# A decoder block in split fp32: another opening order, position rows as matmul rows, and other buffers for the compression's weights

## The chip, the cores and the metric

The kernel runs on one core of one Trainium2 chip. The metric is the device time of one execution in microseconds (us); where several executions were timed it is their median. The core has five engines that run side by side: PE (TensorE, matrix products), ACT (ScalarE), DVE (VectorE), POOL (GpSimd) and SP (SyncE), which here issues all the DMA transfers. A difference of about 0.5% is what repeated runs of this kernel can tell from none.

## What is computed

One layer of a decoder: 512 tokens of width 1024, batch 1. RMS norm, a token mixer, RMS norm and residual, then RMS norm, a SwiGLU channel mixer, RMS norm and residual. The mixer has two head groups that read one combined input projection: four heads of differential attention, and eight query heads (two key/value groups) of native sparse attention with a compressed, a selected and a window branch. Cut to what the change touches:

```python
h = rms_norm(x, attn_pre_norm[l])
proj = h @ w_in                      # dq, dk, dv, nq, kc, vc, ks, vs, kw, vw, gates
...
def compress_tokens(t, tok_idx, pos, w1, w2):
    blocks = t[:, :, tok_idx] + pos          # 31 blocks of 32 tokens, stride 16
    flat = blocks.reshape(..., 32 * 64)
    return silu(flat @ w1) @ w2
...
kc = compress_tokens(kc_tok, tok_idx, k_pos, k_w1, k_w2)
vc = compress_tokens(vc_tok, tok_idx, v_pos, v_w1, v_w2)
```

## The kernel before

**Numbers in two parts.** Most matrix products are done in fp32r on operands that are split in two: hi is the value rounded to fp32r, lo is the rest. A product is then three runs of matmuls: hi by hi, hi by lo, lo by hi. A weight tile is made in three steps: a DMA into a raw tile (`load_w`, L94), a copy on ACT to hi (`to_r`, L99 to L103, whi in the profile) and a subtraction on DVE to lo (`split_w`, L105 to L110, wlo). The raw, hi and lo tiles are 128 by 1024 and come from one shared pool with three buffers of each (`WB`).

**The planner.** The program states data flow; a planner orders the instructions of each engine at compile time by priority (mostly the order of the program text; attention heads are moved up by `HP` = 400) and by when it expects them to be ready, and gives out the buffers of each tag. Engines then run in that fixed order and wait on semaphores. So an edit can change the order of work that it does not mention.

**The opening (L164 to L254).** TensorE first does `WARM` = 12 matmuls on zeros, which no result uses. x comes transposed in eight pieces (`load_x`, L186 to L200): for each a DMA into xraw, an ACT copy scaled by the norm's gain to xh, a DVE operation that makes xl, an ACT square in place, and a DVE add into one of two running sums. Four "k" buffers hold the eight pieces. Among them the raw tiles of the first two weight tiles are loaded (`load_fm`, L202). Then come the constants (identities, masks, `sel`, L214 to L225), the rope tables, and the row scale: `ssum` sums the squares by matmuls, `rsqrt_mean` makes rstd, and `rb` spreads it over the rope tables (L231 to L243).

**The projections.** `fm_tile` (L257) splits a weight tile and does 24 matmuls of 512 columns: whi with the eight xh, whi with the eight xl, wlo with the eight xh. `rope_pair` (L268) does two such tiles and the rotation on DVE. `dv_half` (L327) makes half of the differential values, four tiles of 24 matmuls of 256 columns, evicted with rstd by ACT (L343) and DVE (L344); their PSUM tiles ("mm") have two buffers. `ORDER` (L46) lists the steps: the compressed pair C first, then v1, q0, q1, the value compression cv, n1, k0, the key compression ck, and so on, with the attention heads D0 to D3 and N0 to N7 among the later ones.

**The compression (`compress`, L375 to L458), run for values and keys.** The tokens come as cx, 128 rows (feature, and two neighbours) by 2 groups by 256. For each half of a block DVE adds the position values to 31 windows of 8 steps for each group (L398, 248 elements, reading every eighth element), ACT copies the sum to hi and DVE makes lo (L404 and L405). That gives 16 stationary operands of 124 columns: hi and lo, two groups, 31 blocks. The first weight matrix comes as four tiles through the shared pool (`load_w`, `split_w`), and 32 matmuls of 256 columns accumulate (L414). Two matmuls with `sel`, a stacked identity of 62 columns, add the hi rows to the lo rows and transpose (L420). SiLU and the second matrix follow.

**Attention.** Each softmax map takes its K operand from a "k" buffer (`load_k`, L305, two DMAs), and each head puts its transposed weights into a pair of "pt" tiles (`new_pt`, L504, two buffers of each).

Of the kernel before, what the change touches and what calls it, by code (L numbers as in the profile page):

```python
# [77 lines left out]
def hybrid_block_kernel(  # L78
# [26 lines left out]
    def split_w(raw, w=1024, lo_eng=None, hi_eng="a"):  # L105
        hi = wpool.tile([P, 1024], F32R, tag="hi", name="whi", bufs=WB[1])
        lo = wpool.tile([P, 1024], F32R, tag="lo", name="wlo", bufs=WB[2])
        to_r(hi_eng, hi[:, :w], raw[:, :w])
        (lo_eng or dve).tensor_tensor(lo[:, :w], raw[:, :w], f32(hi[:, :w]), OP.subtract)  # L109
# [28 lines left out]
    sel = T.tile([P, 2 * NCMP], F32, bufs=1, name="sel")  # L138
# [47 lines left out]
    def load_x(k):  # L186
        if k % 2 == 0:
            xraws[k // 2] = T.tile([P, 2, SEQ], F32R, tag="k", name="xraw", bufs=BUFS["k"])
        t = f32(xraws[k // 2][:, k % 2])
        nc.sync.dma_start(t, xT[:, k])  # L190
        h, l = sslot(f"xh{k}"), sslot(f"xl{k}")
        act.activation(h, t, AF.Copy, scale=gc[:, k:k + 1])
# [3 lines left out]
        act.activation(t, t, AF.Square)
        if sqs[k % 2] is None:
            sqs[k % 2] = t
        else:
            dve.tensor_tensor(sqs[k % 2], sqs[k % 2], t, OP.add)  # L200

    def load_fm(m):  # L202
        raws[m] = load_w(wf[m])

    first = 2 * FIRST_PAIR[ORDER.split()[0]]
    load_x(0)
    load_fm(first)
    for k in range(1, 4):
        load_x(k)
    load_fm(first + 1)  # L210
    for k in range(4, NK):
        load_x(k)
# [8 lines left out]
    dve.tensor_copy(sel, cst[:, 3 * P:3 * P + 2 * NCMP])  # L221
# [32 lines left out]
    dve.tensor_scalar_add(lam, lam, -LAM_INIT)  # L254


    def fm_tile(m, lo_eng=None):  # L257
        hi, lo = split_w(raws.pop(m), lo_eng=lo_eng, hi_eng="d" if m // 2 in HIF else "a")
        pt = ps("mm", f"fm{m}")
        seq = [(hi, xh), (hi, xl), (lo, xh)]  # L260
        n = 0
        for w, xx in seq:
            for k in range(NK):
                pe.matmul(pt, w[:, k * P:(k + 1) * P], xx[k], start=(n == 0), stop=(n == 3 * NK - 1))  # L264
# [110 lines left out]
    def compress(d, v, w1, w2, posd, w2cols):  # L375
# [14 lines left out]
        n2 = 2 * NCMP  # L390
        xs = []
        for half in range(2):
            st = tslot("cst", tag="c")
            stv = st[:, :8 * n2].rearrange("p (l g n) -> p l g n", l=8, g=GROUPS)
            for g in range(GROUPS):
                xg = xx[:, g * 256:(g + 1) * 256].rearrange("p (n l) -> p l n", l=8)
                xg = xg[:, :, half:half + NCMP]
                dve.tensor_tensor(stv[:, :, g], xg,  # L398
                                  pos[:, half * 8:half * 8 + 8].unsqueeze(2).to_broadcast([P, 8, NCMP]), OP.add)
            sv = st[:, :8 * n2].rearrange("p (l n) -> p l n", l=8)  # L400
            for q in range(2):
                hv = sslot("chl")[:, :8 * n2].rearrange("p (l s n) -> p l s n", l=4, s=2)
                sq = sv[:, 4 * q:4 * q + 4]
                act.activation(hv[:, :, 0], sq, AF.Copy)  # L404
                dve.tensor_tensor(hv[:, :, 1], sq, f32(hv[:, :, 0]), OP.subtract)  # L405
                xs.append(hv)
        for c in range(4):
            raw = load_w(w1[:, 4 * c:4 * c + 4].rearrange("(a d) l n -> d a (l n)", d=HALF))
            hi, lo = split_w(raw, hi_eng=hie("cv" if v else "ck"))
            for l in range(4):  # L410
                lh = 4 * c + l
                st = xs[lh // 4][:, lh % 4].rearrange("p s n -> p (s n)")
                for wi, w in enumerate((hi, lo)):
                    pe.matmul(hps[:2 * n2, :CMP_HIDDEN], st, w[:, l * 256:(l + 1) * 256],  # L414
                              start=(lh == 0 and wi == 0), stop=(lh == NLH - 1 and wi == 1))
        hs = tslot("chs", tag="c")
        act.activation(hs[:2 * n2, :CMP_HIDDEN], hps[:2 * n2, :CMP_HIDDEN], AF.Copy)
        pt = ps("tr", f"cht{v}")
        for j in range(2):
            pe.matmul(pt[:, j * 64:j * 64 + n2], hs[:2 * n2, j * P:(j + 1) * P], sel[:2 * n2], start=True, stop=True)  # L420
        ptv = pt[:, :P].rearrange("p (j n) -> p j n", j=2)[:, :, :n2]
        e = tslot("ce", tag="c")
        ev = e[:, :P].rearrange("p (j n) -> p j n", j=2)[:, :, :n2]
        act.activation(ev, ptv, AF.Exp, scale=-1.0)
        dve.tensor_scalar_add(ev, ev, 1.0)
        dve.reciprocal(ev, ev)
        if v == 0:
            hT = e[:, 256:256 + P].rearrange("p (j n) -> p j n", j=2)[:, :, :n2]
# [4 lines left out]
            pov = po[:, :n2].rearrange("p (g n) -> p g n", g=GROUPS)  # L433
            z = zero
            for t in (kch, kcl):
                act.activation(t[:, :, NCMP], z[:, :GROUPS], AF.Copy)
            act.activation(kch[:, :, :NCMP], pov, AF.Copy)
            dve.tensor_tensor(kcl[:, :, :NCMP], pov, f32(kch[:, :, :NCMP]), OP.subtract)
        else:
            hT = tslot("chT", tag="c")  # L440
            pool.memset(hT, 0.0)
            hv = hT.rearrange("p (j g r n) -> p j g r n", j=2, g=GROUPS, r=4)
            for j in range(2):
                for g in range(GROUPS):
                    src = (slice(None), j, slice(g * NCMP, (g + 1) * NCMP))
                    bc = [P, 4, NCMP]
                    dve.tensor_tensor(hv[:, j, g, :, :NCMP], ptv[src].unsqueeze(1).to_broadcast(bc),
                                      ev[src].unsqueeze(1).to_broadcast(bc), OP.mult)
# [536 lines left out]
```

## Time and profile before

| | us |
|---|---|
| runs shown: median of 3 (714.56, 717.43, 718.01) | 717.43 |
| profiled execution | 715.25 |
| its span, first to last instruction | 713.2 |
| PE busy | 683.7 |
| DVE busy | 488.3 |
| ACT busy | 295.9 |
| POOL busy | 63.1 |

The span is the part of the profiled execution between the first and the last instruction; 2.05 us of the time lie around it. Busy times are of one engine each and overlap. In the rows of the timeline the first number is the start in us, the second the time that the row covers; "xN" says that N instructions are merged; the brackets give the idle time of the engine ahead of it and what ended that. In the rows of the windows each engine has its busy time and its instructions (x), then come PEclk, the granted TensorE clock as a share of full speed, the share of DMA time used, and GB/s.

### The profile page before, as it was taken

To read this page: it belongs to the slowest core of one execution; us is meant where nothing else is said; L and a number is where in the kernel's file an instruction comes from. 1 tells how busy PE (TensorE), PEld (TensorE's weight loads), DVE (VectorE), ACT (ScalarE), POOL (GpSimd) and SP (SyncE) were. 2 spreads that over 40 slices of the span, in tenths; PEclk is the share of its full clock that TensorE was granted. 3 is DMA by queue.
4 is the path that set the end of the run, shared out by engine and by line. 5 is a ranking of instruction groups with operands and counts; after the bars stand their busy time and mean duration, and the time that the engine had idled before them with its cause. 6 is when DMAs were issued, how large, how long until landed. Compare 5 with 4: busy or idle time off the path is not lost.

```text
span 713.2 us, 9399 instructions
## 1 busy us (share of the span) xinstructions
PE 683.7 (96%) x3536; PEld 566.2 (79%) x3536; DVE 488.3 (68%) x803; ACT 295.9 (41%) x612; POOL 63.1 (9%) x74
## 2 busy tenths in 40 slices
PE   7999999999899998987899999999999999999995
PEld 4888878898788877866888888888888888888884
DVE  5777988876999995669586766867667672222227
ACT  7334444466689965435323233232232321121113
POOL 0000000111745434000000000000000000000000
PEclk8999999999999998999999999999999999999999
DMA  8347878551221300470022332223322222322303
GB/s 311 129 133 244 279 238 298 195 191 45 86 78 60 104 16 30 133 251 30 1 90 88 105 102 89 89 88 93 111 92 89 88 91 94 111 89 88 110 8 119
DMA packets 25980, 83.62 MB, mean 117 GB/s; under 512 B 3408, under 2 KB 4304, under 8 KB 25040
## 3 DMA queue, kind: packets, MB, share of 16 engines
q1 hardware_dynamic: 25936, 83.03, 35.0%
q8 instruction: 28, 0.46, 0.3%
q14 instruction: 16, 0.13, 0.1%
HBM read 73.06 MB, written 9.96 MB: 116 GB/s over the span
## 4 chain that ended last, share of the span: by engine, by line
PE 81%; DVE 12%; ACT 4%; issue 2%; DMA 1%; SPq 0%; DVEq 0%; ACTq 0%
PE gu L835 35%; PE acc L874 15%; PE fm L264 11%; PE tr L489 2%; PE mixp L664 2%; DVE nm L477 2%; PE dv L338 2%; PE vg L360 2%; PE avn L617 2%; PE sc L473 2%; PE sc L474 1%; PE mix L676 1%; PE av L540 1%; DVE p L533 1%; DVE ptl L494 1%
## 5 line engine op out<-in xcount | busy, mean ns | idle before, releaser
L109 DVE TENSOR_TENSOR wlo<-wraw,whi 128x1024 fp32r<-128x1024 f32 (+2 forms) x96 | 116.4, 1214 | 144.8 <-ACT whi L101 95.5
L101 ACT ACTIVATE whi<-wraw 128x1024 fp32r<-128x1024 f32 (+2 forms) x96 | 100.8, 1052 | 215.3 <-PE gu L835 92.0
L835 PE MATMUL gu<-hth,whi 128*128 128x512 f32 (+1 forms) x352 | 86.6, 388 | 0.0
L835 PE MATMUL gu<-htl,whi 128*128 128x512 f32 (+1 forms) x352 | 86.2, 385 | 0.0
L835 PE MATMUL gu<-hth,wlo 128*128 128x512 f32 (+1 forms) x352 | 85.6, 385 | 0.0
L835 PEld LDWEIGHTS gu<-hth,whi 128*128 128x128 f32 x352 | 65.0, 192 | 14.8 <-ACT hth L807 0.3
L835 PEld LDWEIGHTS gu<-htl,whi 128*128 128x128 f32 x352 | 64.3, 188 | 14.7
L835 PEld LDWEIGHTS gu<-hth,wlo 128*128 128x128 f32 x352 | 64.1, 188 | 14.7
L841 DVE RECIPROCAL silu<-silu 128x512 f32<-128x512 f32 (+1 forms) x24 | 74.0, 3085 | 0.7
L498 POOL TENSOR_TENSOR p<-p,l 128x384 f32<-128x384 f32 (+3 forms) x60 | 50.1, 862 | 145.0 <-DVE l L528 88.5
L874 PE MATMUL acc<-whi,ffl 128*128 128x512 f32 x144 | 56.0, 389 | 0.0
L874 PE MATMUL acc<-wlo,ffh 128*128 128x512 f32 x144 | 56.0, 389 | 0.0
L874 PE MATMUL acc<-whi,ffh 128*128 128x512 f32 x144 | 55.9, 389 | 0.0
L479 ACT ACTIVATE p<-sc,nm 128x128 f32<-128x128 f32 (+1 forms) x96 | 50.0, 528 | 10.2 <-DVE nm L477 9.8
L477 DVE TENSOR_REDUCE nm<-sc 128x1 f32<-128x128 f32 (+1 forms) x96 | 42.5, 482 | 11.0 <-PE sc L475 7.8
L264 PE MATMUL fm<-xh,whi 128*128 128x512 f32 x128 | 35.9, 419 | 4.8 <-ACT whi L101 2.9
L493 ACT ACTIVATE pth<-tr 128x384 fp32r<-128x384 f32 (+1 forms) x60 | 31.5, 526 | 17.4 <-PE tr L489 17.2
L473 PE MATMUL sc<-kst,qst 128*128 128x128 f32 (+2 forms) x96 | 35.6, 372 | 1.5 <-DVE pc L574 1.2
L494 DVE TENSOR_TENSOR ptl<-tr,pth 128x384 fp32r<-128x384 f32 (+1 forms) x60 | 34.8, 592 | 3.0 <-ACT pth L493 2.7
L489 PE MATMUL tr<-ident,p 128*128 128x128 f32 x200 | 33.6, 280 | 1.3 <-ACT pct L591 0.7
L264 PEld LDWEIGHTS fm<-xh,whi 128*128 128x128 f32 x128 | 24.9, 199 | 12.3 <-ACT whi L101 5.5
L264 PE MATMUL fm<-xl,whi 128*128 128x512 f32 x128 | 32.6, 391 | 0.0
(219 smaller groups left out, 1186.9 us busy)
## 6 DMA issues: line engine op xcount, KB each, us to landing
wraw<-in_wg SPq DMA_DIRECT2D x22, 512.0 KB, 3.3
wraw<-in_wu SPq DMA_DIRECT2D x22, 512.0 KB, 3.3
wraw<-in_wd SPq DMA_DIRECT2D x22, 512.0 KB, 3.3
wraw<-in_wf SPq DMA_DIRECT2D x16, 512.0 KB, 4.9
qk<-rope SPq DMA_DIRECT2D x7, 1024.0 KB, 5.9
kst<-qk SPq DMA_DIRECT2D x24, 256.0 KB, 4.4
qst<-qk SPq DMA_DIRECT2D x16, 256.0 KB, 2.7
wraw<-in_wo SPq DMA_DIRECT2D x8, 512.0 KB, 4.0
```

Source lines behind the costliest of these rows:

```text
L101: act.activation(dst, src, AF.Copy)
L109: (lo_eng or dve).tensor_tensor(lo[:, :w], raw[:, :w], f32(hi[:, :w]), OP.subtract)
L264: pe.matmul(pt, w[:, k * P:(k + 1) * P], xx[k], start=(n == 0), stop=(n == 3 * NK - 1))
L473: pe.matmul(sv, lhs, kk[:, 0, :w], start=True, stop=False)
L477: dve.tensor_reduce(nm, sv, AX.X, OP.max, negate=True)
L479: act.activation(pt, sv, AF.Exp, bias=nm, accum_out=l[:, i:i + 1])
L489: pe.transpose(tr[:, n * P:(n + 1) * P], pts[i][:, j * P:(j + 1) * P], ident)
L494: dve.tensor_tensor(ptl[:, sl], trv, f32(pth[:, sl]), OP.subtract)
L498: pool.tensor_tensor(p, p, l.to_broadcast(list(p.shape)), OP.mult)
L835: pe.matmul(pt, w_col(ww, k), hx[:, k, s0:s1], start=(n == 0), stop=(n == 3 * NK - 1))
L841: dve.reciprocal(sl, sl)
L874: pe.matmul(acc[i][c], a[f][:, i * P:(i + 1) * P], w[wi][:, c * SEQ:(c + 1) * SEQ], start=(first and n == 0), stop=(last and n == 2))
```

## The change

Three parts.

**The opening.** `load_x` now only loads, makes xh and, after pieces 1 to 3, issues three more matmuls of xh by itself into the warm tile, which no result uses. xl moves to `low_x`, the squares and their sums to a loop of their own, both behind all eight `load_x`. `load_fm` can split a tile when it is loaded, and `rope_pair` and the first two tiles do so. `WARM` goes from 12 to 20. `fm_tile` does whi with xh, wlo with xh, then whi with xl.

**Position rows.** The stationary operand has 128 columns: hi and lo, two groups, 31 blocks and one spare, in which the position values stand. The windows are no longer added to the position values: ACT copies them to hi and DVE makes lo (496 elements each), and the same is done for the position values (16 elements). `sel` now adds the position rows (31 and 95) to every block: it is built from the identity in three DVE operations.

**Weight tiles.** The operands of the compression lie in tiles of the tag "k" (in place of a "c" tile and four "s" tiles), its raw weight tiles too, and hi and lo are a "pt" pair from `new_pt`.

```diff
-WARM = 12
+WARM = 20
+WARMX = 3
...
-        h, l = sslot(f"xh{k}"), sslot(f"xl{k}")
+        h = sslot(f"xh{k}")
         act.activation(h, t, AF.Copy, scale=gc[:, k:k + 1])
-        dve.scalar_tensor_tensor(l, t, gc[:, k:k + 1], f32(h), OP.mult, OP.subtract)
         xh.append(h)
+        if 0 < k < 4:
+            for _ in range(WARMX):
+                pe.matmul(warm_ps, h[:, :P], h, start=True, stop=True)
+
+    def low_x(k):
+        t = f32(xraws[k // 2][:, k % 2])
+        l = sslot(f"xl{k}")
+        dve.scalar_tensor_tensor(l, t, gc[:, k:k + 1], f32(xh[k]), OP.mult, OP.subtract)
         xl.append(l)
+
+    def load_fm(m, split=False):
+        raws[m] = load_w(wf[m])
+        if split:
+            raws[m] = split_w(raws[m])
+
+    first = 2 * FIRST_PAIR[ORDER.split()[0]]
+    load_x(0)
+    load_fm(first, True)
+    for k in range(1, 4):
+        load_x(k)
+    load_fm(first + 1, True)
+    for k in range(4, NK):
+        load_x(k)
+    for k in range(NK):
+        low_x(k)
+    for k in range(NK):
+        t = f32(xraws[k // 2][:, k % 2])
         act.activation(t, t, AF.Square)
-        if sqs[k % 2] is None:
-            sqs[k % 2] = t
+        if k < 2:
+            sqs[k] = t
         else:
             dve.tensor_tensor(sqs[k % 2], sqs[k % 2], t, OP.add)
...
-    dve.tensor_copy(sel, cst[:, 3 * P:3 * P + 2 * NCMP])
+    n2 = GROUPS * NPAD
+    dve.tensor_tensor(sel, ident[:, :n2], ident[:, n2:], OP.add)
+    for r in (NCMP, n2 + NCMP):
+        dve.tensor_tensor(sel, sel, ident[:, r:r + 1].to_broadcast([P, n2]), OP.add)
...
-    def fm_tile(m, lo_eng=None):
-        hi, lo = split_w(raws.pop(m), lo_eng=lo_eng, hi_eng="d" if m // 2 in HIF else "a")
+    def fm_tile(m):
+        hi, lo = raws.pop(m)
         pt = ps("mm", f"fm{m}")
-        seq = [(hi, xh), (hi, xl), (lo, xh)]
+        seq = [(hi, xh), (lo, xh), (hi, xl)]
...
             if m not in raws:
-                load_fm(m)
+                load_fm(m, True)
...
-            st = tslot("cst", tag="c")
-            stv = st[:, :8 * n2].rearrange("p (l g n) -> p l g n", l=8, g=GROUPS)
-            for g in range(GROUPS):
-                xg = xx[:, g * 256:(g + 1) * 256].rearrange("p (n l) -> p l n", l=8)
-                xg = xg[:, :, half:half + NCMP]
-                dve.tensor_tensor(stv[:, :, g], xg,
-                                  pos[:, half * 8:half * 8 + 8].unsqueeze(2).to_broadcast([P, 8, NCMP]), OP.add)
-            sv = st[:, :8 * n2].rearrange("p (l n) -> p l n", l=8)
-            for q in range(2):
-                hv = sslot("chl")[:, :8 * n2].rearrange("p (l s n) -> p l s n", l=4, s=2)
-                sq = sv[:, 4 * q:4 * q + 4]
-                act.activation(hv[:, :, 0], sq, AF.Copy)
-                dve.tensor_tensor(hv[:, :, 1], sq, f32(hv[:, :, 0]), OP.subtract)
-                xs.append(hv)
+            st = T.tile([P, 2, SEQ], F32R, tag="k", name="cst", bufs=BUFS["k"])
+            st = st.rearrange("p q (l s g n) -> p (q l) s g n", s=2, g=GROUPS, n=NPAD)
+            xg = xx.rearrange("p (g n l) -> p l g n", g=GROUPS, l=8)[:, :, :, half:half + NCMP]
+            pg = pos[:, half * 8:half * 8 + 8].unsqueeze(2).to_broadcast([P, 8, GROUPS])
+            for dst, src in (((slice(0, NCMP)), xg), (NCMP, pg)):
+                act.activation(st[:, :, 0, :, dst], src, AF.Copy)
+                dve.tensor_tensor(st[:, :, 1, :, dst], src, f32(st[:, :, 0, :, dst]), OP.subtract)
+            xs.append(st)
         for c in range(4):
-            raw = load_w(w1[:, 4 * c:4 * c + 4].rearrange("(a d) l n -> d a (l n)", d=HALF))
-            hi, lo = split_w(raw, hi_eng=hie("cv" if v else "ck"))
+            raw = f32(T.tile([P, 2, SEQ], F32R, tag="k", name="w1", bufs=BUFS["k"])).rearrange("p a b -> p (a b)")
+            nc.sync.dma_start(raw, w1[:, 4 * c:4 * c + 4].rearrange("(a d) l n -> d a (l n)", d=HALF))
+            hi, lo = (t.rearrange("p a b -> p (a b)")[:, :1024] for t in new_pt())
+            to_r("a", hi, raw)
+            dve.tensor_tensor(lo, raw, f32(hi), OP.subtract)
...
-                    pe.matmul(hps[:2 * n2, :CMP_HIDDEN], st, w[:, l * 256:(l + 1) * 256],
+                    pe.matmul(hps[:, :CMP_HIDDEN], st, w[:, l * 256:(l + 1) * 256],
```

The remaining lines of the diff carry the width of 64 columns (two groups of 32) in place of 62 through the rest of `compress`.

More of the change, by code (lines that the diff above doesn't have):

```diff
@@ L137, in hybrid_block_kernel @@
     cmask_b = T.tile([P, NT * NPAD], BF16, bufs=1, name="cmask_b")
-    sel = T.tile([P, 2 * NCMP], F32, bufs=1, name="sel")
+    sel = T.tile([P, 2 * NPAD], F32, bufs=1, name="sel")
     valid = T.tile([P, 1], F32, bufs=1, name="valid")
@@ L190, in load_x @@
         nc.sync.dma_start(t, xT[:, k])
-        h, l = sslot(f"xh{k}"), sslot(f"xl{k}")
+        h = sslot(f"xh{k}")
         act.activation(h, t, AF.Copy, scale=gc[:, k:k + 1])
-        dve.scalar_tensor_tensor(l, t, gc[:, k:k + 1], f32(h), OP.mult, OP.subtract)
         xh.append(h)
-        xl.append(l)
+        if 0 < k < 4:
[5 more added lines that the diff above has]
+        dve.scalar_tensor_tensor(l, t, gc[:, k:k + 1], f32(xh[k]), OP.mult, OP.subtract)
+        xl.append(l)
+    def load_fm(m, split=False):
[14 more added lines that the diff above has]
+        t = f32(xraws[k // 2][:, k % 2])
         act.activation(t, t, AF.Square)
-        if sqs[k % 2] is None:
-            sqs[k % 2] = t
+        if k < 2:
+            sqs[k] = t
         else:
             dve.tensor_tensor(sqs[k % 2], sqs[k % 2], t, OP.add)
[L202 to L212, printed above, removed]
     cst = tslot("cst", tag="o")
@@ L389, in compress @@
         hps = ps(CMPT, f"cmp{v}")
-        n2 = 2 * NCMP
+        n2 = GROUPS * NPAD
         xs = []
         for half in range(2):
-            st = tslot("cst", tag="c")
-            stv = st[:, :8 * n2].rearrange("p (l g n) -> p l g n", l=8, g=GROUPS)
-            for g in range(GROUPS):
-                xg = xx[:, g * 256:(g + 1) * 256].rearrange("p (n l) -> p l n", l=8)
-                xg = xg[:, :, half:half + NCMP]
-                dve.tensor_tensor(stv[:, :, g], xg,
-                                  pos[:, half * 8:half * 8 + 8].unsqueeze(2).to_broadcast([P, 8, NCMP]), OP.add)
-            sv = st[:, :8 * n2].rearrange("p (l n) -> p l n", l=8)
-            for q in range(2):
-                hv = sslot("chl")[:, :8 * n2].rearrange("p (l s n) -> p l s n", l=4, s=2)
-                sq = sv[:, 4 * q:4 * q + 4]
-                act.activation(hv[:, :, 0], sq, AF.Copy)
-                dve.tensor_tensor(hv[:, :, 1], sq, f32(hv[:, :, 0]), OP.subtract)
-                xs.append(hv)
@@ L410, in compress @@
             for l in range(4):
                 lh = 4 * c + l
-                st = xs[lh // 4][:, lh % 4].rearrange("p s n -> p (s n)")
+                st = xs[lh // 8][:, lh % 8].rearrange("p s g n -> p (s g n)")
                 for wi, w in enumerate((hi, lo)):
-                    pe.matmul(hps[:2 * n2, :CMP_HIDDEN], st, w[:, l * 256:(l + 1) * 256],
+                    pe.matmul(hps[:, :CMP_HIDDEN], st, w[:, l * 256:(l + 1) * 256],
                               start=(lh == 0 and wi == 0), stop=(lh == NLH - 1 and wi == 1))
@@ L416, in compress @@
         hs = tslot("chs", tag="c")
-        act.activation(hs[:2 * n2, :CMP_HIDDEN], hps[:2 * n2, :CMP_HIDDEN], AF.Copy)
+        act.activation(hs[:, :CMP_HIDDEN], hps[:, :CMP_HIDDEN], AF.Copy)
         pt = ps("tr", f"cht{v}")
         for j in range(2):
-            pe.matmul(pt[:, j * 64:j * 64 + n2], hs[:2 * n2, j * P:(j + 1) * P], sel[:2 * n2], start=True, stop=True)
-        ptv = pt[:, :P].rearrange("p (j n) -> p j n", j=2)[:, :, :n2]
+            pe.matmul(pt[:, j * 64:j * 64 + n2], hs[:, j * P:(j + 1) * P], sel, start=True, stop=True)
@@ L422, in compress @@
+        ptv = pt[:, :P].rearrange("p (j n) -> p j n", j=2)
         e = tslot("ce", tag="c")
-        ev = e[:, :P].rearrange("p (j n) -> p j n", j=2)[:, :, :n2]
+        ev = e[:, :P].rearrange("p (j n) -> p j n", j=2)
         act.activation(ev, ptv, AF.Exp, scale=-1.0)
@@ L427, in compress @@
         if v == 0:
-            hT = e[:, 256:256 + P].rearrange("p (j n) -> p j n", j=2)[:, :, :n2]
+            hT = e[:, 256:256 + P].rearrange("p (j n) -> p j n", j=2)
             dve.tensor_tensor(hT, ptv, ev, OP.mult)
@@ L432, in compress @@
                 pe.matmul(po[:, :n2], w2t[:, j], hT[:, j], start=(j == 0), stop=(j == 1))
-            pov = po[:, :n2].rearrange("p (g n) -> p g n", g=GROUPS)
+            pov = po[:, :n2].rearrange("p (g n) -> p g n", g=GROUPS)[:, :, :NCMP]
             z = zero
@@ L444, in compress @@
                 for g in range(GROUPS):
-                    src = (slice(None), j, slice(g * NCMP, (g + 1) * NCMP))
+                    src = (slice(None), j, slice(g * NPAD, g * NPAD + NCMP))
                     bc = [P, 4, NCMP]
```

## The prediction

> **What bounds the kernel now.** I read the page's busy shares first, to see which engine is the bound, and then a table of stages (windows), to see where that engine stands idle or slow.
>
> ```profile
> span 713.2 us, 9399 instructions
> PE 683.7 (96%) x3536; PEld 566.2 (79%) x3536; DVE 488.3 (68%) x803; ACT 295.9 (41%) x612; POOL 63.1 (9%) x74
> core 0: us, PE busy (x) PEld busy (x) DVE busy (x) ACT busy (x) POOL busy (x), PEclk, DMA share, GB/s
> 0.00:7.65 7.65, 4.18 (x13) 1.43 (x13) 1.12 (x6) 3.42 (x6) 0.20 (x4) 0.99 0.69 201
> 7.65:15.49 7.84, 6.71 (x14) 3.94 (x15) 7.22 (x13) 7.84 (x14) 0.00 (x0) 0.57 1.05 397
> 15.49:23.50 8.01, 8.01 (x37) 6.67 (x37) 7.18 (x16) 5.37 (x8) 0.00 (x0) 1.00 0.74 265
> 23.50:38.35 14.85, 14.14 (x119) 13.94 (x120) 11.04 (x23) 3.74 (x9) 0.00 (x0) 1.00 0.24 72
> 38.35:110.00 71.65, 69.75 (x348) 58.77 (x347) 58.85 (x89) 31.20 (x47) 0.52 (x1) 1.00 0.71 235
> 110.00:180.00 70.00, 69.78 (x477) 61.55 (x475) 54.44 (x119) 37.73 (x108) 9.38 (x12) 1.00 0.50 174
> 180.00:260.00 80.00, 75.87 (x519) 61.34 (x519) 75.35 (x188) 65.07 (x196) 41.60 (x46) 0.98 0.24 77
> 260.00:350.00 90.00, 79.64 (x443) 67.91 (x442) 67.30 (x146) 43.43 (x103) 11.43 (x12) 0.94 0.26 88
> ```
>
> TensorE is busy 683.7 of 713.2 us, and no other engine above 488.3. So an edit is worth the TensorE idle or slow time that it removes, 29.5 us at most. The table says where that lies: before 7.65; in the opening, where ACT is busy all 7.84 us, DVE 7.22 and the granted clock is only 0.57; 0.71 us in 23.5 to 38.35; 1.9 us in 38.35 to 110. From 110 to 180 there is 0.2 us. The 14.5 us between 180 and 350 are in code that the diff leaves alone.
>
> **The opening.** Rows of the timeline, by time (start, us, engine, line, operation), then of the matmuls' line L264 and of the tile xraw (min/median/max ns, first and last start). Here x arrives in eight pieces, and the first two weight tiles (fm_a, fm_b: 48 matmuls) are multiplied with it.
>
> ```profile
> 1.22 4.18 PE L174 MATMUL warm<-warm 128*128 128x512 bf16 x12 [1.22 <-DVE zero L225]
> 7.65 0.79 PE L264 MATMUL fm<-xh,whi 128*128 128x512 f32 x1 [2.25 <-ACT whi L101]
> 8.02 1.93 ACT L192 ACTIVATE xh<-xraw,gc 128x512 fp32r<-128x512 f32 x3
> 10.38 1.04 ACT L101 ACTIVATE whi<-wraw 128x1024 fp32r<-128x1024 f32 x1
> 14.73 0.71 ACT L192 ACTIVATE xh<-xraw,gc 128x512 fp32r<-128x512 f32 x1
> 21.50 1.99 PE L264 MATMUL fm<-xh,wlo 128*128 128x512 f32 x8
> L264 PE MATMUL fm<-xh,whi x16: 389/628/793, 7.6 to 17.0; 128*128 128x512 f32 x16
> L264 PE MATMUL fm<-xl,whi x16: 389/389/389, 15.8 to 21.3; 128*128 128x512 f32 x16
> L264 PE MATMUL fm<-xh,wlo x16: 389/389/398, 19.5 to 23.1; 128*128 128x512 f32 x16
> L190 SPq DMA_DIRECT2D xraw<-in_xT x8: 328/432/738, 1.2 to 6.5; - x8
> DMA to landing us min/median/max: 3.5/5.8/6.3
> L196 ACT ACTIVATE xraw<-xraw x8: 613/614/633, 7.5 to 18.0; 128x512 f32<-128x512 f32 x8
> ```
>
> The last piece of x lands by 6.5 + 6.3 = 12.8 us, but ACT makes its xh only at 14.73 to 15.44: ACT spent five squares of 0.61 us ahead of it. From 15.8 on TensorE runs the 16 with xl, the 16 with wlo and, at 17.0, the last of the 16 of whi with xh: 33 of the 48, back to back until 23.49, 0.232 us each.
>
> The change puts the squares behind all of xh. ACT then needs after xh3 (third of the row at 8.02, now free to end near 9.6) one whi, 1.04, and four xh at some 0.62: 3.5 us. The second whi is begun at 10.38 today, so its data is there by then: started between 9.6 and 10.38, the four end between 13.1 and 13.9. The landing bound is 12.8 + 0.71 = 13.5, which I take: **13.5**. So xh is complete 1.9 us sooner, and the new order (whi with xh, wlo with xh, whi with xl) leaves more that needs no xl.
>
> How much is done by 13.5? TensorE has 5.85 us from 7.65, or 25 slots of 0.232. Nine go to the new warm matmuls (three after each of x1 to x3); some two are lost before xh1. That leaves 15, as many as before did by 15.8. The remaining 33 take 7.7 us again and end at 21.2 instead of 23.49: **-2.3 us**. Bounds: strictly in program order, only 8 of fm_a are done at 13.7 and 40 remain, 23.0 (-0.5); packed without a gap, 48 + 9 slots from 7.65 end at 20.9 (-2.6).
>
> This count needs TensorE at full clock from 7.65. The granted clock by windows:
>
> ```profile
> 4.12:7.53 3.41, 1.28 (x6) 0.39 (x4) 0.75 (x1) 1.71 (x3) 0.00 (x0) 1.00 0.95 339
> 7.53:10.95 3.42, 2.81 (x4) 1.14 (x4) 3.21 (x4) 3.42 (x7) 0.00 (x0) 0.50 1.04 407
> 10.95:14.36 3.41, 2.88 (x7) 2.31 (x8) 2.90 (x4) 3.41 (x7) 0.00 (x0) 0.50 1.06 398
> 307.91:311.32 3.41, 2.04 (x11) 1.66 (x10) 1.26 (x3) 1.18 (x4) 0.00 (x0) 1.00 0.94 292
> ```
>
> The clock is full from 4.12 to 7.53, in which TensorE is busy only 1.28 us, and halved for the next 6.8 us. A later window with 2.04 us busy (307.91) is in the full clock, and no drop follows it. The twelve warm matmuls end at 5.40: that fits seven at a cold 0.43 until 4.2 and five at some 0.22. With 20 of them thirteen follow the seven and end near 7.0: 2.8 us busy in that window, above the 2.04 that held. I take the clock as kept. [...]
>
> [...]
>
> **What the squares leave late.** The row scale rstd needs the sums of squares, and DVE is the tight engine:
>
> ```profile
> 19.03 1.89 DVE L200 TENSOR_TENSOR xraw<-xraw 128x512 f32<-128x512 f32 x3
> 23.32 0.84 PE L234 MATMUL ssum<-ones,xraw 128*128 128x1 f32 x7
> 34.95 0.48 DVE L344 SCALAR_TENSOR_TENSOR dv<-dv,rstd,dv 128x256 fp32r<-128x256 f32 x1
> 35.49 0.74 PE L338 MATMUL dv<-whi,xh 128*128 128x256 f32 x4 [0.71 <-DVE dv L344]
> L221 DVE COPY sel<-cst 128x62 f32<-128x62 f32 x1 | 0.2, 191 | 0.0
> ```
>
> Up to 20.9 DVE has the same xl, wlo, constants and adds in both kernels, plus two small operations for sel (about 0.4 us by the 191 ns row), and it is 91% busy (7.22 + 7.18 of 15.85). So the adds still end at 20.9 to 21.3. Before, the ssum matmuls waited for TensorE until 23.3. Now TensorE is ready at 21.2, when the adds are: the chain to rstd, rb and the eviction of dv moves with it, and the stall of 0.71 at 35.49 stays (bounds: gone, or grown by the whole 2.3). I take 0. ACT's eight squares, 4.9 us, lie behind xh from 13.5 beside two whi of wdv and end near 20.5, ahead of the last add.
>
> On SP the DMAs of x, weights and constants keep their order, and none gets a new wait. The new order within fm_tile holds whi for eight matmuls longer (1.9 us); its buffer is one of three, next needed two tiles (11 us) on: 0.
>
> **The compression.** It runs twice, once near 44 to 68 us and once near 85 to 98.
>
> ```profile
> L414 PE MATMUL cmp<-wlo,chl x32: 276/279/380, 60.4 to 96.9; 128*124 128x256 f32 x32
> 62.93 0.38 PE L414 MATMUL cmp<-wlo,chl 128*124 128x256 f32 x1 [0.53 <-DVE wlo L109]
> 91.39 0.73 PE L264 MATMUL fm<-xh,whi 128*128 128x512 f32 x2 [1.37 <-DVE chl L405]
> L398 DVE TENSOR_TENSOR cst<-cx,pos x8: 612/629/637, 44.3 to 88.1; 128x248 f32<-128x248 f32 x8
> L404 ACT ACTIVATE chl<-cst x8: 395/405/416, 45.5 to 89.0; 128x248 fp32r<-128x248 f32 x8
> L405 DVE TENSOR_TENSOR chl<-cst,chl x8: 404/410/418, 47.7 to 91.9; 128x248 fp32r<-128x248 f32 x8
> 103.48 4.96 SPq L310 DMA_DIRECT2D kst<-qk  x8
> 110.12 0.22 PE L473 MATMUL sc<-kst,qst 128*128 128x128 f32 x1
> ```
>
> Its matmuls keep their number and columns (124 stationary columns become 128), so their time. TensorE stood 0.53 us for a wlo and 1.37 us for a chl, both made by DVE. Per compression DVE did 4 x 0.63 + 4 x 0.41 = 4.2 us. Now it does two subtractions of 496 elements and two of 16. By sel's row (L221) 62 elements take 0.19, by L405 248 read in order take 0.41: 1.2 ns each above 0.12. By L398 248 read 8 apart take 0.63, 2.05 ns each. So 496 elements cost 0.7 or, read 8 apart as they are, 1.1 us, and 16 cost 0.15. Sum 2 x 1.1 + 2 x 0.15 = 2.5: some 1.6 us less on DVE. ACT did 4 x 0.405 = 1.6 and now does four copies, 1.6 to 2.6; it is 31.2 of 71.65 us busy, so that hides (without that cover, 1.0 us per compression).
>
> [...]
>
> The weight tiles move from the shared three-deep buffers to the four "k" and two pairs of "pt", idle until the first attention head's loads at 103.48. So they can be loaded and split early, and no projection tile waits behind them. I take 1.4 of the 1.9 us: **-1.4** (bounds 0 and -1.9; three quarters, since the larger stall is the one whose DVE work shrinks most).
>
> Sum: -2.3 - 1.4 + 0 = **-3.7 us**. The profiled execution took 715.25 (span 713.2 and 2.05 around it), so the sum by it is 711.5. It lies 2.2 below the median of 717.43 of the runs shown; I place the forecast from the middle of the two, 716.3: 716.3 - 3.7 = **712.6**.
>
> **The rivals.** *DVE keeps the opening.* If the planner lets the wlo of the next tiles ahead of the adds, rstd and rb come no earlier than before, DVE evicts dv at 34.95 as now, and the matmul at 35.49 starts at 35.49: 2.3 are given back as a longer stall. For it: DVE at 91%. Against: the ssum matmuls had 2.1 us to spare. Time 716.3 - 1.4 = 714.9.
>
> [...]
>
> *Slower: attention's K tiles come late.* They share the "k" buffers with the compression's two operand tiles and four weight tiles. Today all eight loads go out from 103.48, after the compression's last matmul at 96.9, and the scores begin at 110.12. The slack is 6.5 us: from the point where the planner ends the second compression later than 103.5, each us holds up the heads, whose DVE work is 75.35 of 80 us busy from 180 to 260 and cannot catch up. Put off behind one projection pair (48 x 0.232 = 11 us) it costs 11 - 6.5 = 4.5, about the gains; behind two, 22 - 6.5 = 15.5, and 716.3 - 3.7 + 15.5 = 728. The latter is this rival. Against: its tiles are ready earlier than before.
>
> *A new order downstream.* The planner orders all engines anew, and 14.5 us of idle between 180 and 350 can move. If a third goes: 707.8.
>
> **How the numbers follow.** Forecast 0.52, DVE 0.20, clock 0.08, late K 0.07, new order 0.13. The forecast's own range is 710.1 (715.25 - 2.6 - 1.9 - 0.7) to 715.8 (716.3 - 0.5). New order reaches below it, DVE with an unlucky start above it: all but 2 in 10 lies in 707 to 717.5. A measurement of this kernel tells about 0.5% from no change, here 3.6 us, so faster means below 713.8: four fifths of the forecast (0.41), the new order (0.13), half of clock (0.04) and a tenth of DVE (0.02) make 0.60. Slower, above 721, is late K: 0.07. The rest is 0.33.
>
> **What would show it.** xh complete near 13.5 and the last fm_b matmul near 21.2 (opening; 23 refutes it); granted clock 1.0 from 4 to 24; dv's last tile starting near 33.2 rather than 35.49 (DVE rival: 35.5); no idle above 0.5 us at the compression's matmuls; DVE's strided subtraction near 1.1 us; scores starting by 107 (late K: after 112). It would be wrong if TensorE idles more between 180 and 350 than the 14.5 us of now.

## The result, and the profile after

The changed kernel is slower: 725.75 us (median of 4 runs, 724.17 to 727.08) against 717.27 (4 runs), a ratio of 1.0124 with a 95% interval of 1.0095 to 1.0152. The forecast was 712.6 with a range of 707 to 717.5. The profiled execution took 724.17.

The page of the changed kernel, its span and busy shares:

```profile
span 722.2 us, 9431 instructions
PE 690.2 (96%) x3553; PEld 569.4 (79%) x3553; DVE 490.4 (68%) x797; ACT 299.9 (42%) x612; POOL 62.3 (9%) x74
```

Its windows, with the columns of the prediction's table (us, busy time of PE, PEld, DVE, ACT, POOL with instructions, granted clock, DMA share, GB/s; PEld is TensorE's loading of its stationary operands):

```profile
7.65:15.49 7.84, 7.73 (x34) 5.70 (x33) 5.44 (x7) 7.45 (x13) 0.00 (x0) 1.00 1.05 396
15.49:23.50 8.01, 7.78 (x40) 6.38 (x39) 8.01 (x22) 5.72 (x11) 0.00 (x0) 1.00 0.79 275
23.50:38.35 14.85, 14.85 (x120) 14.49 (x119) 12.62 (x28) 5.40 (x10) 0.00 (x0) 1.00 0.24 72
38.35:110.00 71.65, 69.09 (x338) 56.87 (x337) 54.98 (x78) 31.23 (x44) 0.53 (x1) 1.00 0.75 251
180.00:260.00 80.00, 72.22 (x477) 59.09 (x475) 67.72 (x171) 59.79 (x175) 33.64 (x38) 0.94 0.21 64
260.00:350.00 90.00, 82.05 (x450) 67.44 (x448) 71.00 (x151) 48.05 (x119) 15.84 (x16) 0.94 0.28 100
```

The opening does what it was meant to: the clock is full where it was 0.57, and the stall in 23.5 to 38.35 is gone. From 180 to 260 TensorE issues 477 matmuls where it issued 519. That is where the time went, and no line of the diff is there. TensorE idles 15.7 us between 180 and 350 where it idled 14.5, but this window no longer holds the same work.

To place the loss, cut the span at two points that both kernels have: the start of the last matmul of the last projection (the tile vg) and the first matmul of the channel mixer (gu). First and last starts, before and then after:

```profile
L360 PE MATMUL vg<-wlo,xh x32: 285/292/375, 149.2 to 171.2; 128*128 128x280 f32 x32
L835 PE MATMUL gu<-hth,ws x64: 277/283/415, 331.5 to 361.7; 128*128 128x256 f32 x64
```

```profile
L377 PE MATMUL vg<-wlo,xh x32: 288/292/377, 149.0 to 168.3; 128*128 128x280 f32 x32
L849 PE MATMUL gu<-hth,ws x64: 277/280/583, 341.1 to 371.7; 128*128 128x256 f32 x64
```

The front is 2.9 us shorter, the stretch between them (the attention heads) 12.5 us longer, 172.8 for 160.3, and the tail as long as it was (713.2 - 331.5 = 381.7 against 722.2 - 341.1 = 381.1). Windows over just that stretch, before and then after:

```profile
171.20:331.50 160.30, 147.67 (x904) 120.60 (x902) 134.82 (x326) 108.27 (x303) 57.15 (x63) 0.97 0.26 85
```

```profile
168.30:341.10 172.80, 154.35 (x920) 124.99 (x917) 142.21 (x331) 111.70 (x307) 56.82 (x63) 0.95 0.25 83
```

TensorE's idle time there grows from 12.6 to 18.5 us (+5.8). Its busy time grows by 6.7: 16 matmuls more, which the front no longer does (16 x 0.163 = 2.6 at the old mean), and the rest slower ones, 0.168 us each, at a clock of 0.95 for 0.97. So most of the front's 2.9 is displaced work. The groups of instructions from 180 to gu name the idle: the score matmuls before, then after (busy, mean ns, then idle ahead of them and what ended it), and the one long wait ahead of 180 in the timeline after:

```profile
L473 PE MATMUL sc<-kst,qst 128*128 128x384 f32 (+3 forms) x63 | 24.3, 386 | 1.5 <-DVE pc L574 1.2
```

```profile
L487 PE MATMUL sc<-kst,qst 128*128 128x128 f32 (+1 forms) x64 | 25.1, 392 | 6.2 <-ACT p L493 5.6
...
179.45 1.22 PE L567 MATMUL rsb<-ident,rs 128*128 128x128 f32 x8 [2.74 <-DVE rs L128]
```

That is 4.7 + 2.7 us of new idle time, less 1.6 in other groups. The first is a wait that hardly was there before: TensorE waits to start a score tile until ACT has made the weights p of an earlier one. The waits from 193 to 243 us, in the middle of the heads (engine, what waits, for whom: total, times, longest), show the ring that this belongs to. Here sc and tr are the scores and transposes of a map, scc and trc those of the compressed branch. First before, then after, each with its window:

```profile
193.00:243.00 50.00, 49.26 (x357) 41.00 (x358) 47.12 (x129) 44.75 (x137) 25.66 (x31) 1.00 0.28 88
...
ACT pth L493 <- PE tr L489: 2.1, 4, 0.7
...
PEld sc L473 <- ACT p L479: 0.7, 4, 0.2
```

```profile
193.00:243.00 50.00, 45.80 (x314) 37.33 (x313) 42.32 (x111) 38.95 (x113) 21.62 (x26) 0.97 0.23 69
...
ACT pth L507 <- PE tr L503: 6.6, 9, 2.4
...
DVE ptl L508 <- ACT pth L507: 5.1, 3, 4.2
PEld sc L487 <- ACT p L493: 4.0, 6, 1.7
...
PE sc L487 <- ACT p L493: 2.5, 3, 1.5
ACT p L493 <- DVE nm L491: 2.4, 3, 1.4
```

A softmax map runs score (PE), maximum nm (DVE), p (ACT), transpose tr (PE), hi pth (ACT), lo ptl (DVE). Before, TensorE was busy 49.26 of these 50 us and DVE 47.12, and the engines of this chain waited for little. After, each engine waits for the one ahead in the chain, in turn, and none is as full as it was: TensorE 45.80, DVE 42.32. The operations are the same; the order in which the fixed queues hold them is not. TensorE issues the first transposes of the compressed weights of heads N0 to N6 after 36, 44, 51, 59, 68, 75 and 84 maps before, and after 34, 40, 48, 54, 61, 72 and 79 now.

### The profile page after: what moved, and what is told of

The parts are those of the page before. It is cut to its first block, busy times and chain, and to the rows that moved or that the text cites. A ratio compares the mean times of both kernels' runs of the same rounds, so it can differ in the third digit from the quotient of the medians.

```text
span 722.2 us, 9431 instructions
## 1 busy us (share of the span) xinstructions
PE 690.2 (96%) x3553; PEld 569.4 (79%) x3553; DVE 490.4 (68%) x797; ACT 299.9 (42%) x612; POOL 62.3 (9%) x74
## 4 chain that ended last, share of the span: by engine, by line
PE 77%; DVE 12%; ACT 4%; issue 3%; DMA 3%; POOL 1%; SPq 0%; DVEq 0%; POOLq 0%; ACTq 0%
PE gu L849 34%; PE acc L888 15%; PE fm L281 8%; PE dv L355 3%; PE mixp L678 3%; PE vg L377 2%; PE tr L503 2%; PE avn L631 2%; PE sc L487 2%; PE sc L488 1%; DVE nm L491 1%; ACT p L493 1%; PE av L554 1%; PE mix L690 1%; DMA w<-in_kw 1%
## 5 line engine op out<-in xcount | busy, mean ns | idle before, releaser
L110 DVE TENSOR_TENSOR wlo<-wraw,whi 128x1024 fp32r<-128x1024 f32 (+2 forms) x88 | 106.7, 1213 | 141.8 <-ACT whi L102 94.4
L102 ACT ACTIVATE whi<-wraw 128x1024 fp32r<-128x1024 f32 (+2 forms) x88 | 92.5, 1051 | 193.3 <-PE gu L849 92.5
L487 PE MATMUL sc<-kst,qst 128*128 128x128 f32 (+1 forms) x96 | 36.2, 378 | 6.2 <-ACT p L493 5.6
L281 PE MATMUL fm<-xh,whi 128*128 128x512 f32 x128 | 33.7, 397 | 0.4 <-DVE rope L300 0.2
L281 PE MATMUL fm<-xh,wlo 128*128 128x512 f32 x128 | 33.0, 392 | 0.0
```

Of the source, the lines that this page charges most:

```text
L102: act.activation(dst, src, AF.Copy)
L487: pe.matmul(sv, lhs, kk[:, 0, :w], start=True, stop=False)
```

## The experiments

Two theories. **Order** (theory A in the forecasts below): the planner, fed other costs and buffers, put the heads' steps into another order, which exposes the chain; the parts of the change themselves do no harm there. **Parts**: some resource that the change takes (the opening's split at load, the "k" or "pt" tiles) holds up the heads. The measure besides the time is the period of a head: the starts of the compressed scores of N2 and N6 in the timeline, over four. It is 10.7 us before and 12.9 after. The last column is the start of the last vg matmul against before's 171.2.

| run | ratio to before (95%) | us | period | end of vg against before |
|---|---|---|---|---|
| after | 1.0124 (1.0095 to 1.0152) | 725.75 | 12.9 | -2.9 |
| e_open | 1.0042 (1.0024 to 1.0059) | 719.01 | 10.7 | +5.1 |
| e_open_rows | 1.0011 (0.9993 to 1.0029) | 717.03 | 10.7 | +2.9 |
| e_bufs | 1.0091 (1.0064 to 1.0117) | 722.06 | 10.9 | +7.9 |
| e_comp | 1.0018 (1.0006 to 1.0030) | 717.68 | 11.0 | +1.7 |
| a_k_only | 1.0214 (1.0182 to 1.0245) | 730.97 | 12.5 | +5.6 |
| a_seq_old | 1.0043 (1.0025 to 1.0062) | 719.21 | 10.7 | +4.1 |
| a_k1_first | 0.9926 (0.9902 to 0.9949) | 710.65 | 10.7 | -2.3 |
| b_k1_first | 1.0122 (1.0098 to 1.0145) | 725.24 | 13.1 | -2.6 |
| k1_nowarm | 1.0000 (0.9988 to 1.0011) | 716.84 | 10.7 | +1.0 |
| k1_warmx0 | 0.9987 (0.9968 to 1.0007) | 715.58 | 11.0 | -0.5 |
| k1_o5 | 1.0091 (1.0071 to 1.0111) | 722.43 | 12.0 | -2.5 |

The kernel before, run beside them, took 716.06 (the two e_open, e_bufs and a_k_only), 716.09 (e_comp, a_seq_old and the two k1_first) and 717.12 (last three); the ratios compare each run with its own.

The last column compares like with like only where the front holds the same work. After and a_k_only move some 16 matmuls behind it, b_k1_first 27.

By their times, few of the runs came out as the order theory forecast. b_k1_first and e_comp did. e_bufs did too, but by luck: its loss was forecast between 170 and 350 us and lies in the front. e_open, e_open_rows and a_seq_old came out slower than forecast, by 2.0 us at most, and a_k_only by 4.0; a_k1_first was 1.4 us faster. k1_nowarm, k1_warmx0 and k1_o5 were slower than anything forecast for them. What bears the order theory out is the period of a head: 10.7 to 11.0 us where the maps run as far ahead as in before (in e_bufs to within one map), and 12.5 to 13.1 where they do not. k1_o5 is the exception.

**The parts one by one.** e_open is before with the hunks of the opening alone (`WARM`, `load_x`, `low_x`, the split at load, the order in `fm_tile`):

```diff
-WARM = 12
+WARM = 20
+WARMX = 3
...
-                load_fm(m)
+                load_fm(m, True)
```

> The opening alone (20 warm matmuls, three more after each of x1 to x3, xl and squares moved back, whi-wlo-xl order), the compression as before. Theory A, the order of attention is what cost the time: TensorE's order from the first score on is that of before here, so the end of the projections comes 1 to 2 us sooner and the time is 714 to 717, a ratio of 0.995 to 1.000. [...]

e_open_rows adds the position rows and the operands in "k" tiles, with the weight tiles left in the shared pool:

```diff
-            st = tslot("cst", tag="c")
+            st = T.tile([P, 2, SEQ], F32R, tag="k", name="cst", bufs=BUFS["k"])
```

> The opening and the position rows, with the operands in the k tiles, but the weight tiles of the compression in the shared pool as before. TensorE's order of the attention steps is again that of before. Theory A: 713 to 717, since all that differs from after is the weight tiles' buffers. [...]

e_bufs is before with only the weight tiles moved:

```diff
-            raw = load_w(w1[:, 4 * c:4 * c + 4].rearrange("(a d) l n -> d a (l n)", d=HALF))
-            hi, lo = split_w(raw, hi_eng=hie("cv" if v else "ck"))
+            raw = f32(T.tile([P, 2, SEQ], F32R, tag="k", name="w1", bufs=BUFS["k"])).rearrange("p a b -> p (a b)")
+            nc.sync.dma_start(raw, w1[:, 4 * c:4 * c + 4].rearrange("(a d) l n -> d a (l n)", d=HALF))
+            hi, lo = (t.rearrange("p a b -> p (a b)")[:, :1024] for t in new_pt())
+            to_r("a", hi, raw)
+            dve.tensor_tensor(lo, raw, f32(hi), OP.subtract)
```

> The weight tiles alone: raw tiles in the k buffers and hi and lo in pt pairs, the opening and the position sums as before. The order of the attention steps on TensorE is another than in before and after. Theory A: some 3 to 12 us slower than before, with the loss between 170 and 350 us, 720 to 729. [...]

a_k_only is after with hi and lo of those tiles from the shared pool:

```diff
-            hi, lo = (t.rearrange("p a b -> p (a b)")[:, :1024] for t in new_pt())
-            to_r("a", hi, raw)
-            dve.tensor_tensor(lo, raw, f32(hi), OP.subtract)
+            hi, lo = split_w(raw, hi_eng=hie("cv" if v else "ck"))
```

> After, but hi and lo of the compression's weights from the shared pool; only the raw tiles are in the k buffers. The order of the attention steps on TensorE is that of after. Theory A: as slow as after, 723 to 727. Rival D, the pt tiles themselves (their release late for the first heads) cost it: 713 to 717.

No part alone slows the heads: the period is 10.7 with the opening, 10.7 with opening and rows, and 10.9 with the weight tiles moved. It is 12.5 without the "pt" tiles but with the rest, so it is not those tiles that hold up the heads. What the parts lose, they lose in the front, and what a_k_only loses beyond after is there too. The timeline of e_open, and the waits of e_bufs from 38 to 130 us:

```profile
64.60 3.60 PE L278 MATMUL fm<-xh,whi 128*128 128x512 f32 x8 [3.54 <-ACT whi L102]
95.15 3.46 PE L278 MATMUL fm<-xh,whi 128*128 128x512 f32 x8 [1.82 <-ACT whi L102]
```

```profile
PE cmp L417 <- DVE chl L405: 6.4, 1, 6.4
```

In e_open, where tiles are split as they are loaded, a projection waits 5.4 us for whi near the two compressions. a_k_only waits there too, 4.78 and 3.25 us, and after does not: the two differ in whether hi and lo of the compression's weights come from the shared pool. So it is these tiles, in a pool of three buffers, that make the projection wait. With the weight tiles moved and the operands in their old tiles (e_bufs), it is the operand chl that TensorE waits 6.4 us for; why, no run shows.

**The order, from both sides.** a_seq_old is after with the old order within a tile, e_comp the compression's parts on the old opening (so the diff of `compress` and `sel` without the opening's hunks):

```diff
-        seq = [(hi, xh), (lo, xh), (hi, xl)]
+        seq = [(hi, xh), (hi, xl), (lo, xh)]
```

> After, but fm_tile keeps its old order (whi with xh, whi with xl, wlo with xh); the same instructions otherwise. Nothing of the attention is edited, but the planner's order of it is again the one with the scores far ahead: 36, 44, 51, 59, 68, 75 and 84 score tiles are issued at the compressed branch of heads 0 to 6, as in before, where after has 34, 40, 48, 54, 61, 72 and 79. Theory A (scores less far ahead cost the 10 us): 712 to 718, the heads' period near 10.7 us instead of 12.9. Rival C (buffers or other parts of the change cost it): 722 to 728.

> The compression's two parts alone (position rows, operands and weights in the k and pt tiles), the opening as before. The planner's order has the scores far ahead (36, 44, 51, 59, 68, 75, 84). Theory A: the heads' period near 10.7 us and the time of before or a little less, 714 to 718. Rival C: 722 to 728.

a_k1_first and b_k1_first swap two neighbouring steps of `ORDER` in after and in before, the key compression and the second differential key pair. Both lie ahead of the heads N0 to N7, and the swap adds and removes no operation:

```diff
-    "C v1 q0 q1 cv n1 k0 ck k1 n0 s W0 v0 g W4 D0 D1 W1 N0 W2 N1 N2 W3 N3 N4 N5 N6 W5 W7 D2 M0 W6 M1 M2 "
+    "C v1 q0 q1 cv n1 k0 k1 ck n0 s W0 v0 g W4 D0 D1 W1 N0 W2 N1 N2 W3 N3 N4 N5 N6 W5 W7 D2 M0 W6 M1 M2 "
```

> After with two steps swapped in the list of steps (k1 ahead of the key compression ck), the same instructions otherwise. The planner's order has the scores far ahead again (36, 44, 51, 59, 68, 75, 84). Theory A: 712 to 718, period near 10.7 us. Rival C: 722 to 728.

> Before with the same swap (k1 ahead of ck): nothing of the change is in it, but the planner now has the scores less far ahead (33, 40, 48, 57, 64, 72, 82). Theory A: slower than before by about as much as after is, 722 to 728, period 12 to 13 us. Rival C: 716 to 719, as before.

This is the decisive pair. The swap takes 15.1 us from after (about 14 by the ratios) and adds 9.2 to before. A cost of the swap itself cannot have both signs, though a small one beside the rest is not excluded. What it does in both is to throw the planner from one order into the other. With the swap, after's maps at the transposes are before's (36, 44, 51, ...), and before's become 33, 40, 48, 57, 64, 72, 82. Windows from vg to gu and from 193 to 243 us, then waits from 193 to 243, first of a_k1_first, then of b_k1_first:

```profile
168.90:330.40 161.50, 148.84 (x905) 122.03 (x903) 133.47 (x327) 107.83 (x303) 56.38 (x63) 0.96 0.25 85
193.00:243.00 50.00, 49.51 (x360) 40.99 (x359) 46.59 (x130) 44.16 (x134) 24.60 (x29) 1.00 0.25 77
```

```profile
168.60:339.20 170.60, 155.40 (x931) 126.42 (x929) 142.69 (x331) 111.26 (x309) 57.54 (x63) 0.95 0.25 83
193.00:243.00 50.00, 44.28 (x282) 36.69 (x282) 42.96 (x106) 34.54 (x104) 21.00 (x24) 0.90 0.21 67
```

```profile
ACT pth L507 <- PE tr L503: 3.0, 5, 1.0
```

```profile
ACT pth L493 <- PE tr L489: 9.3, 9, 2.3
...
PE scc L565 <- ACT p L479: 3.3, 4, 1.3
PE trc L589 <- DVE ptl L494: 3.0, 2, 2.8
```

The good order has the whole change in it and runs as before (161.5 us, 12.7 idle); the bad one has none of it and shows the same ring of waits. (27 matmuls more lie in the long stretch of b_k1_first, some 4.5 of the 10.3 us by which it is longer than before's; the period does not depend on them.) a_k1_first is also faster than both kernels, 710.65 us. a_seq_old and e_comp, whose heads come out in the good order too, have periods of 10.7 and 11.0. What the planner changes is its whole plan, the order and with it which buffer each tile gets; no run separates the two.

**What the warm matmuls are worth.** With the good order of the heads the opening's matmuls can be taken out. k1_nowarm and k1_warmx0 are a_k1_first with the old twelve, and without the nine between the first pieces of x:

```diff
-WARM = 20
-WARMX = 3
+WARM = 12
+WARMX = 0
```

```diff
-WARMX = 3
+WARMX = 0
```

> The kernel with k1 ahead of ck, but with the 12 warm matmuls of before and none after x1 to x3; the planner's order of the heads is the same. Theory A says nothing of it; the clock step of the prediction does: the clock halves again from 7.5 to 14.4, some five matmul slots are not made up, 711.5 to 713. Rival E, the row scale's chain (sums of squares on DVE, rstd, eviction of dv) hides the matmuls: 710 to 711.5, no difference from the same kernel with them.

> The same with the 20 warm matmuls but none after x1 to x3. If the clock holds on the 20 alone, 710 to 711.5, and up to nine slots come free before xh is complete, so the first pair ends as early or up to 1 us earlier. If it halves at 10.9, because few matmuls run from 7.5 on, 711.5 to 713.

Windows of k1_nowarm, and the timeline of k1_warmx0:

```profile
7.65:15.49 7.84, 6.21 (x14) 4.08 (x15) 5.45 (x7) 7.46 (x13) 0.00 (x0) 0.67 1.05 393
15.49:23.50 8.01, 8.01 (x34) 6.49 (x33) 7.73 (x20) 3.31 (x6) 0.00 (x0) 0.89 0.74 263
23.50:38.35 14.85, 13.00 (x93) 12.46 (x92) 8.29 (x22) 4.62 (x10) 0.00 (x0) 0.89 0.23 72
```

```profile
31.14 2.08 PE L257 MATMUL rb<-ident,rstd 128*128 128x128 f32 x8 [1.39 <-DVE rstd L128]
...
40.44 1.89 PE L281 MATMUL fm<-xh,whi 128*128 128x512 f32 x7 [1.03 <-DVE dv L361]
```

Without them the whole gain is gone: 0.74%, or 5.3 us by the ratios, with an interval of about 1.9 to either side. The clock is 0.67 as xh arrives and 0.89 from 23.50 to 38.35: in k1_nowarm TensorE waits 1.39 us for rstd at 33.86 (the row rb), and the next fours of dv matmuls take 1.20, 1.05 and 0.92 us where later ones take 0.64. Without the nine alone most of it is gone as well, though the clock is then full from 7.65 to 15.49 all the same (1.00), and the first dv matmul starts at 22.08, as in after (21.99): the loss comes later, in the two stalls shown, the first of them where rb stands ahead of its rstd. k1_nowarm has this stall as well; a_k1_first, with all the warm matmuls, does not. These two runs thus price the matmuls together with the order that goes with them, not the clock alone.

**Is it how far ahead the scores run?** In the bad orders fewer maps are issued ahead of each transpose. k1_o5 is a_k1_first with D0 ahead of the output weights W4 and W1 ahead of D1, which by the compiled order issues 38, 44, 52, 60, 67, 76 and 84:

```diff
-n0 s W0 v0 g W4 D0 D1 W1 N0
+n0 s W0 v0 g D0 W4 W1 D1 N0
```

> K1 ahead of ck, and the first output weight tile loaded between the heads D0 and D1 (two tokens of the list of steps moved). The planner's order has the scores still a little further ahead at the first heads (38, 44, 52, 60, 67, 76, 84 instead of 36, 44, 51, 59, 68, 75, 84). Theory A: the heads' period cannot fall much below 10.7 us, since DVE is then busy nearly all the time; 708 to 712. If the lead alone set the period, it would fall to 10 and the time to below 708.

It missed: a period of 12.0 and 722.43 us. The window of 193 to 243 in its profile (an execution of 728.63, 6 us above its median, so its sizes, the period of 12.0 too, are to be read with care):

```profile
193.00:243.00 50.00, 45.81 (x316) 37.07 (x314) 43.07 (x112) 39.85 (x120) 24.58 (x28) 0.97 0.19 55
```

The scores are as far ahead as in the good order, and the heads are nearly as slow as in the bad one; the median, too, is 11.8 us above a_k1_first's. So that count is a mark of the two orders of the other runs, not the cause. Which feature of an order exposes the chain stays open.

## Why the prediction was wrong

**The step that failed** is one sentence on the bound: the 14.5 us of idle between 180 and 350 "are in code that the diff leaves alone". They are, but the planner orders that code anew. The rival "A new order downstream" said so and was priced in one direction only, as a gain ("If a third goes: 707.8"), with 0.13. The same mechanism had a loss to give: from 180 to 260 TensorE was busy 75.87 and DVE 75.35 of 80 us, in an order that left few waits, so that another order had more to lose than to gain there (an argument after the event; that the order did it is shown by the pair of swaps). The stretch of the heads grew by 12.5 us, of which some 2.6 are work displaced from the front. The prediction's own sign of being wrong, more than 14.5 us of idle time between 180 and 350, came: 15.7. The slower rival, late K tiles, did not happen: the scores start at 106.2, where 107 was named as its test.

**Opening, -2.3.** Near in the end, with some luck. xh was complete at 13.7 (forecast 13.5). The last fm_b matmul ended at 21.75 rather than 21.2, so the opening itself gave 1.7 us. The tile of dv that started at 35.49 now starts at 33.37 (forecast 33.2), but 0.7 of these 2.1 us are the stall ahead of it, which the sum left in place, and 0.2 went to a new wait at 21.99. The forecast's own count was high as well: 25 slots less nine and two leave 14, not 15. From the timeline of after:

```profile
1.22 7.00 PE L175 MATMUL warm<-warm 128*128 128x512 bf16 x20 [1.22 <-DVE zero L242]
...
8.00 0.50 PE L281 MATMUL fm<-xh,whi 128*128 128x512 f32 x1
...
11.15 2.55 ACT L193 ACTIVATE xh<-xraw,gc 128x512 fp32r<-128x512 f32 x4
...
19.10 2.65 PE L281 MATMUL fm<-xl,whi 128*128 128x512 f32 x11
...
21.99 0.74 PE L355 MATMUL dv<-whi,xh 128*128 128x256 f32 x4 [0.23 <-ACT craw L297]
...
33.37 0.64 PE L355 MATMUL dv<-whi,xh 128*128 128x256 f32 x4
```

The twenty warm matmuls run to 8.2 and not to 7.0, and the first fm matmul starts at 8.00 where it started at 7.65, which is 0.35 of the 0.55 by which fm_b is late. The forecast let seven of them be cold, up to 4.12, as in the profile of before. In this execution twelve started 0.43 us apart, and the trace's first entry of the granted clock, 1.00, begins at 6.33 (in before at 4.12). In a_k1_first, whose front does the same work as before's but for one matmul (3536 - 904 against 3553 - 905, of which 17 are warm ones), the start of the last vg matmul is 2.3 us earlier.

**The clock.** It was kept, as forecast: 1.00 from 7.65 to 38.35. But the ground given, more busy time than the 2.04 us that held, was too thin: in the same profile of before the window from 270.37 to 273.78 has TensorE busy 2.38 us, and the clock was 0.50 behind it, from 273.78 to 277.20. Also, the bound of 29.5 us counts idle time alone; slow time (a clock of 0.57 from 7.65 to 15.49) stands in the busy 683.7. The chances hold 0.08 for a clock that falls in the opening in spite of the twenty warm matmuls. No run shows that: it was 1.00 from 7.65 to 15.49 in after, a_k_only, e_open, a_seq_old, a_k1_first and k1_warmx0, which have them. What a run shows is the opening without them: in k1_nowarm the clock there was 0.67 and the loss about 5.3 us, orders and the stall behind 23.5 included.

**Stall at 35.49, 0.** Wrong by its 0.7: it went. The planner put ssum between the tiles of dv, and rb at 29.6, and nothing waited. The opening alone did not remove it (e_open: 0.94 us at 34.15); with the position rows beside it (e_open_rows) it was gone as well.

**Held whi, 0.** Right in after, but for another reason than the one named. "Its buffer is one of three, next needed two tiles on" does not hold near the compressions: e_open waited 5.4 us there, and a_k_only 8.0. What covers it is that the hi and lo tiles of the compression's weights leave the shared pool in the same change.

**Compression, -1.4.** Wrong. The DVE operations came as forecast (1.133 and 0.19 us against 1.1 and 0.15); the ACT copies took 1.168 and 0.224, 2.8 us per compression, above the 2.6 of the upper bound. By the tile cst of after:

```profile
L415 ACT ACTIVATE cst<-pos x4: 208/224/233, 20.9 to 81.7; 128x16 fp32r<-128x16 f32 x4
L416 DVE TENSOR_TENSOR cst<-pos,cst x4: 176/190/226, 22.5 to 83.3; 128x16 fp32r<-128x16 f32 x4
L415 ACT ACTIVATE cst<-cx x4: 1107/1168/1195, 46.3 to 80.7; 128x496 fp32r<-128x496 f32 x4
L416 DVE TENSOR_TENSOR cst<-cx,cst x4: 1131/1133/1176, 47.5 to 82.3; 128x496 fp32r<-128x496 f32 x4
```

But the idle time did not go, and that is outside the term's bounds of 0 and -1.9: TensorE idles 2.56 us from 38.35 to 110 where it idled 1.9. (The matmuls themselves kept their time, as forecast: 0.279 us at the median with 124 stationary columns, 0.281 with 128.) In the timeline of after it waits for the new lo tiles:

```profile
87.24 0.38 PE L428 MATMUL cmp<-ptl,cst 128*128 128x256 f32 x1 [1.32 <-DVE ptl L423]
...
96.14 0.39 PE L428 MATMUL cmp<-ptl,cst 128*128 128x256 f32 x1 [0.55 <-DVE ptl L423]
```

DVE's lo is still the last to come, for a weight tile now instead of an operand. The working asked what DVE saves and not what it does last. e_comp, the compression's parts alone, shows no gain either: +1.3 us (0.4 to 2.1).

**The sum.** With the heads in the good order a_k1_first gains 0.74% (0.51 to 0.98), about 5.3 us, where the sum said 3.7. How much of that is the change alone is not shown. a_k1_first has the swap in its front as well, and between the two profiled executions only 3.0 us of span lie (713.2 and 710.2), 2.3 of them in the front. a_seq_old also has the good order of the heads and is 0.43% slower than before: its front is 4.1 us longer, with a wait of 1.38 us for rstd at 30.91 and a clock of 0.89 from 23.50 to 38.35 (four dv matmuls took 1.05 us from 32.79 on, 0.64 from 35.94 on). So the order of the front counts beside that of the heads. Nor is the gain the sum of parts: e_open loses 3.0 us, e_comp 1.3.

## What to carry to other kernels

Where a compiler orders the engines, an edit's price has two terms: what it does, and what the new order does to stages that it never touches; in a stage where the engines are nearly full and wait little, as here, the second term has more room on the loss side. Look for it first in the count of instructions per stretch (here 519 against 477), then in the waits: here a ring in which every engine waits for the next came and went with the order, whether the change's buffers were in use or not. Before a change is dropped for such a loss, swap two independent steps in the changed kernel and in the old one; if that moves the loss from one to the other, it is the order that has to be chosen, and the change is to be judged in a good one.

## What the runs showed of the hardware

- Reading every eighth element took ACT as long as DVE: the 496 of cst took 1.168 us on ACT and 1.133 on DVE. In order, 512 took ACT 0.64 (three xh in 1.93), and in before 248 took 0.405 on ACT and 0.410 on DVE, against 0.629 on DVE when read eight apart (L398). The rows of ACT do not separate the reads from the writes, which go out in runs of 31 elements.
- In two places of after, slow time follows a wait. Behind the wait of 2.74 us at 179.45 TensorE was busy throughout the next ten microseconds, but at a granted clock of 0.66; behind one of 1.45 us at 230.59 the clock from 232 to 234 was 0.50. The windows of after:

```profile
180.00:190.00 10.00, 10.00 (x55) 8.93 (x54) 7.94 (x19) 5.15 (x15) 4.86 (x5) 0.66 0.09 27
...
232.00:234.00 2.00, 2.00 (x7) 1.52 (x6) 0.53 (x3) 1.79 (x7) 1.27 (x2) 0.50 0.00 0
```

Such time counts as busy, and so it is part of the 4.1 us (6.7 - 2.6) by which the busy time of the heads grew beyond the displaced work. TensorE was busy 0.96 of the 3.41 us up to 180.41 (the length of the windows in the prediction) and 1.87 of the 3.41 us up to 231.61, and in the next 3.41 us the clock was 0.50 both times. Busy time alone does not tell the outcome: in before the clock was 0.50 behind a window with 2.38 us busy (from 270.37) and 1.00 behind one with 2.04 (from 307.91). What sets it is not shown.
